# A gated hybrid layer on one core: memory tokens as the first stage, x normalized before its only split, cross heads ahead of causal heads

## The chip, the core and the metric

The kernel runs on one of the eight cores of a Trainium2 chip. TensorE (PE in the profile, its weight loads PEld) multiplies; VectorE (DVE), ScalarE (ACT) and GpSimd (POOL) do the rest; SyncE (SP) issues nearly all the DMAs. Each engine takes its own instructions in the order in which the program emits them and waits on semaphores for the others. The metric is the device time of one execution in microseconds (us), and less is better.

## The reference

One decoder layer with three parallel branches, for 256 tokens `x` and 256 memory tokens `mem`, 1024 channels each, all float32:

```python
h = rms_norm(x, norm_g)
(qa, ka, va, ga, ub, vb, gb, qc, gc, ma, mb, mc) = split_cols(h @ w_in, IN_SPLITS)
out_a = moba_attention(rope(qa), rope(ka), va) * silu(ga)            # 6 causal heads x 128
out_b = ub * (tril(w_spatial) @ layer_norm(vb) + b_spatial) * silu(gb)   # 6 groups, chunks of 128 tokens
mem_n = rms_norm(mem, mem_norm_g)
mk, mv = split(mem_n @ w_mem_kv)
out_c = softmax(qc @ mk.T * scale) @ mv * silu(gc)                   # 4 cross heads x 128
y = (sigmoid(ma) * (out_a @ w_branch_a) + sigmoid(mb) * (out_b @ w_branch_b)
     + sigmoid(mc) * (out_c @ w_branch_c))
return rms_norm(x + y @ w_out, final_norm_g)
```

With 256 tokens and blocks of 256 the block-sparse attention is one causal block for each head.

## The kernel before, in words

**Arithmetic.** Nearly every product is made of three matmuls on numbers of reduced width (`mm3`, L343): an operand is split into a high part, rounded on ScalarE, and a low part, the rest, on VectorE, and high x high, high x low and low x high are summed in PSUM.

**Chunks.** All weights pass through TensorE as 106 chunks of 128x1024, two of which make a piece of 1 MB that is one load (L168 to L176). `plan` (L46) gives the order of the first 82. A *token* chunk (vvb, mv, sig; `mm_tok`) holds two k-slices of 512 columns and takes 12 matmuls; four of them make one group of 512 output columns with tokens on the partitions. A *feature* chunk (q, k, qc, gc, ub, ga, gb, mk; `mm_fea`, matmuls on L435) holds all eight k-slices of 128 columns and takes 16 matmuls; its result has features on the partitions. vvb is the causal heads' v beside the gMLP's v, sig the merge gates. Then come 16 chunks of branch projections (`mm_br`) and 8 of the output projection (`mm_out`).

**Loop.** The loop at L983 runs over the chunks. In turn `c` it first emits side work (`U.slot(c, False)`), then the split of chunk `c + 3` (`split`: high part L184, low part L188), maybe a load on SP, then the matmuls of chunk `c`, and then side work for TensorE (`U.slot(c, True)`). Raw pieces have three buffers, split chunks four.

**Planner.** `Units` (L68) holds the side work as units with an engine, a supposed duration, what they come after, and a due turn. It keeps a supposed clock for each engine. A unit is emitted when it seems ready and its engine is not too far ahead of TensorE, or at the latest in its due turn. It sets only the order of emission; what really holds an engine is the semaphores.

**First stage.** L224 to L228 load `xw`: for each of eight k-slices, 256 columns of transposed x and 512 of weights (ten DMAs, `st` tiles). L229 to L237 then load pieces 2 and 3 and x by rows (`load_x`). The lines 307 to 319 multiply x by its gain without its norm, split that as `hh`, `hl`, and split the weights; the first four chunks, vvb 0, run on these (L375). The rows' norm comes from the squares of x (`xsq0`, `xsq1`, L268), square root, reciprocal, two diagonals that two matmuls with a matrix of ones spread over the partitions (`rms_all`, L288), and a copy to SBUF. For vvb it is applied when the sums leave PSUM (`evict_v`). For all later chunks GpSimd multiplies transposed x by it (`nm0` to `nm7`, L516), and each k-slice is split a second time with the gain (`nxh`, `nxl`).

**Memory tokens.** They are loaded after x's norm is known (`load_mem`), split with their gain in units `mxh`, `mxl`, and used by mk and mv as chunks 46 to 53; their norm is applied to mk by a multiplication (`mkf`) and to mv when it leaves PSUM.

**Heads.** Each head is a chain of units: scores on TensorE, maximum on VectorE, exponent on ScalarE, normalization, a turn of the weights (by VectorE's 32x32 transposes for causal heads 2 and 3 and cross heads 0 to 2, L571, on TensorE for the others), split, product with v, copy. `back` lets a head start only when the third head before it is normalized. Six causal heads come first, then four cross heads.

Of the kernel before, what the change touches and what calls it, by code (L numbers as in the profile page):

```python
# [45 lines left out]
def plan():  # L46


    p = [("vvb", g) for g in range(3)]
    for r in range(3):  # L50
        p += [(n, h) for h in (2 * r, 2 * r + 1) for n in ("q", "k")]
        p += ([("sig", 0)], [("gc", h) for h in range(HC)], [("ga", h) for h in range(4)])[r]
        p += [("ub", 2 * r + i) for i in range(2)]
    p += [(n, h) for n in ("qc", "mk") for h in range(HC)]
    p += [("mv", 0), ("sig", 1)]
    p += [("ga", h) for h in range(4, HA)]
    p += [("gb", g) for g in range(GB)]
# [70 lines left out]
def tile_hybrid_layer(ctx: ExitStack, tc: tile.TileContext, xw, memT, mem, x, fin_g, ln_g, w, w_sp, b_sp, rope, out):  # L128
# [108 lines left out]
    load_x()  # L237

# [27 lines left out]
    def row_squares(src, acc, junk):  # L266

        nc.scalar.activation(junk, src, AF.Square, accum_out=acc)  # L268
# [38 lines left out]
    for k in range(KD):  # L307
        c, a, g = k // 2, (k % 2) * 512, gain[:, k:k + 1]
        if k in (0, 2):

            nc.vector.tensor_scalar(hh[:, k, :], x_k(k), g, None, op0=OP.mult)
        elif k < 4:
            gain_hi(x_k(k), g, hh[:, k, :])
        for o, e in (((0, 256), (256, 512)) if k == 0 else ((0, 512),)):
            nc.scalar.activation(hi[c][:, a + o:a + e], st_k(k, S + o, S + e), AF.Copy)  # L315
# [44 lines left out]
    def mm_tok(c):  # L360
        _, name, o, k0 = chunks[c]
        sh, sl = {"mv": ("mh", "ml"), "sig": ("nh", "nl")}.get(name, (None, None))
        sh, sl = (V[sh], V[sl]) if sh else (hh, hl)
# [18 lines left out]
        if k0 + 2 == KD and name == "vvb":  # L382
            U.add(f"vvb.{o}", ACT, 1.6, lambda: evict_v(o), after=[f"vvb.{o - 512}" if o else "xrow", f"c{c}"],
                  first=True)
# [12 lines left out]
        elif k0 + 2 == KD:  # L397
            slot_tile("mvl", [128, 2, CW], "mr0", F32R)
            for t in range(2):
                p, f = acc[name, o][t], rstm[:, t:t + 1]  # L400
                h, l = V["cx"][:, 2, 2 * t:2 * t + 2, :].rearrange("p a b -> p (a b)"), V["mvl"][:, t, :]
                nc.scalar.activation(h, p, AF.Copy, scale=f)
                U.run(ACT, 0.62, U.end[f"c{c}"])
                later(f"mvl{t}", DVE, 0.7, scaled_lo, l, p, f, h, due=c + 2)
            U.end[f"{name}.{o}"] = U.end[f"c{c}"]

    def evict_v(o):
# [708 lines left out]
```

## Time and profile before

| | |
|---|---|
| time, two runs | 325.04 and 324.62 us, median 324.83 us |
| span of the profiled execution, first to last instruction | 323.3 us |
| the profiled execution's own time | not given apart from its span; the runs' median stands 1.5 us above the span |
| busy: TensorE, weight loads | 315.8 us (98%), 268.9 us (83%) |
| busy: VectorE, ScalarE, GpSimd | 246.6 us (76%), 202.5 us (63%), 40.1 us (12%) |
| moved by DMA | 64.92 MB, mean 201 GB/s, 400 to 430 GB/s from 8 to 26 us |
| mean granted TensorE clock | 0.998 |

The profile is of one execution. A row of a listing in order of time gives start, duration, engine, line, operation, the tile written and the tiles read, shapes, count, and in brackets how long the engine stood idle before it and what ended that. A row of waits gives waiter and releaser, then total, times and longest in us. A row of windows gives the stretch, then busy time of TensorE, weight loads, VectorE, ScalarE and GpSimd with instruction counts, the granted clock, the DMA's busy share and its GB/s.

### The profile page before, as it was taken

Reading aid. Unit: us, or ns where it says so; the run is one execution under the profiler, and the core shown is the slowest. Engines: PE = TensorE matmul, PEld = TensorE weight load, DVE = VectorE, ACT = ScalarE, POOL = GpSimd, SP = SyncE. Lnnn points to the kernel's source line nnn. Section 1 sums busy time; section 2 is a strip of 40 time slices with the busy share of each in tenths; the row PEclk is TensorE's granted clock in tenths of the full one; section 3 lists DMA queues with packets and bytes.
Section 4 is the critical chain, followed back from the end, with each engine's and each line's share of the span. In section 5 each row is a group of like instructions: output and inputs, shape, how many; then the busy total and the mean of one; then the engine's idle time right before and its main releaser. Section 6 shows DMA issues by size and latency. Waiting matters only on the chain.

```text
span 323.3 us, 4570 instructions
## 1 busy us (share of the span) xinstructions
PE 315.8 (98%) x1644; PEld 268.9 (83%) x1644; DVE 246.6 (76%) x419; ACT 202.5 (63%) x346; POOL 40.1 (12%) x42
## 2 busy tenths in 40 slices
PE   8999999999999999999999999999999999999992
PEld 3788888888888888898888888888888888888982
DVE  3969956985876999898979639989857659769452
ACT  4879887556865555557677698576746633434433
POOL 1007420000000000030200009200124000000022
PEclk9999999999999999999999999999999999999999
DMA  7999796555327565554544533864640667463003
GB/s 246 419 426 398 258 363 220 216 194 216 136 78 302 172 180 208 164 192 138 185 151 176 195 130 131 312 233 170 208 182 19 244 231 289 150 241 130 0 2 130
DMA packets 13846, 64.92 MB, mean 201 GB/s; under 512 B 1792, under 2 KB 2944, under 8 KB 8576
## 3 DMA queue, kind: packets, MB, share of 16 engines
q1 hardware_dynamic: 13536, 64.31, 55.1%
q10 hardware_dynamic: 288, 0.33, 0.3%
q8 instruction: 13, 0.21, 0.2%
q14 instruction: 9, 0.07, 0.1%
HBM read 62.79 MB, written 1.05 MB: 197 GB/s over the span
## 4 chain that ended last, share of the span: by engine, by line
PE 96%; DMA 2%; ACT 1%; SPq 0%; ACTq 0%; issue 0%; DVE 0%
PE acc L435 36%; PE acc L344 13%; PE acc L345 13%; PE acc L346 13%; PE aux L344 5%; PE aux L345 5%; PE aux L346 5%; PE acc L375 3%; DMA st<-in_xw_dram 2%; PE aux L579 1%; PE aux L814 1%; PE aux L626 0%; PE aux L674 0%; SPq L218 0%; ACT hi L315 0%; PE aux L288 0%
## 5 line engine op out<-in xcount | busy, mean ns | idle before, releaser
L188 DVE TENSOR_TENSOR lo<-raw,hi 128x1024 fp32r<-128x1024 f32 x102 | 130.2, 1280 | 43.0 <-ACT hi L184 42.0
L184 ACT ACTIVATE hi<-raw 128x1024 fp32r<-128x1024 f32 x102 | 107.6, 1056 | 44.3 <-PE acc L346 29.6
L435 PE MATMUL acc<-n,hi 128*128 128x512 f32 x304 | 78.5, 394 | 0.0
L435 PEld LDWEIGHTS acc<-n,hi 128*128 128x128 f32 x304 | 54.8, 189 | 9.5
L435 PEld LDWEIGHTS acc<-n,lo 128*128 128x128 f32 x304 | 41.5, 190 | 3.0
L435 PE MATMUL acc<-n,lo 128*128 128x256 f32 x304 | 42.4, 282 | 0.0
L344 PE MATMUL acc<-hi,n 128*128 128x512 f32 x80 | 31.5, 394 | 0.0
L345 PE MATMUL acc<-lo,n 128*128 128x512 f32 x80 | 31.2, 390 | 0.0
L346 PE MATMUL acc<-hi,n 128*128 128x512 f32 x80 | 31.2, 389 | 0.0
L571 DVE STREAM_TRANSPOSE mid<-p 32x128 f32<-32x128 f32 (+1 forms) x80 | 23.1, 289 | 1.6 <-ACT p L609 0.5
L741 POOL TENSOR_TENSOR vb<-vb,lng 128x768 f32<-128x768 f32 x2 | 4.6, 2276 | 108.4 <-DMA raw<-in_w_dram 94.7
L346 PEld LDWEIGHTS acc<-hi,n 128*128 128x128 f32 x80 | 15.0, 188 | 3.2
L345 PEld LDWEIGHTS acc<-lo,n 128*128 128x128 f32 x80 | 15.0, 188 | 2.9
L344 PEld LDWEIGHTS acc<-hi,n 128*128 128x128 f32 x80 | 15.0, 188 | 2.9
L958 POOL TENSOR_TENSOR xk<-xk,fing 128x512 f32<-128x512 f32 (+1 forms) x4 | 4.0, 1013 | 68.0 <-ACT jk L954 68.0
L516 POOL TENSOR_TENSOR st<-st,bc 128x256 f32<-128x256 f32 x8 | 9.1, 1170 | 24.4 <-ACT bc L293 24.4
L439 ACT ACTIVATE qk<-acc 128x256 f32<-128x256 f32 x12 | 4.6, 380 | 10.7 <-PE acc L435 10.6
L439 ACT ACTIVATE jt<-acc 128x256 f32<-128x256 f32 x14 | 5.3, 377 | 9.0 <-PE acc L435 8.9
L825 POOL TENSOR_TENSOR qk<-qk,ga 128x512 f32<-128x512 f32 x3 | 5.8, 1966 | 33.8 <-ACT ga L801 33.8
L375 PE MATMUL acc<-hi,h 128*128 128x512 f32 (+1 forms) x34 | 8.9, 386 | 0.9 <-ACT hi L315 0.9
L344 PE MATMUL acc<-hi,a 128*128 128x512 f32 x24 | 9.4, 393 | 0.0
L346 PE MATMUL acc<-hi,a 128*128 128x512 f32 x24 | 9.3, 389 | 0.0
(233 smaller groups left out, 601.2 us busy)
## 6 DMA issues: line engine op xcount, KB each, us to landing
raw<-in_w_dram SPq DMA_DIRECT2D x39, 1024.0 KB, 4.9
raw<-in_w_dram SPq DMA_DIRECT2D x24, 512.0 KB, 4.6
st<-in_xw_dram SPq DMA_DIRECT2D x6, 384.0 KB, 7.2
xk<-in_x_dram SPq DMA_DIRECT2D x2, 1024.0 KB, 9.1
mt<-in_memT_dram SPq DMA_DIRECT2D x2, 512.0 KB, 7.8
mm<-in_mem_dram SPq DMA_DIRECT2D x2, 512.0 KB, 9.8
out_dram<-xk SPq DMA_DIRECT2D x4, 256.0 KB, 2.7
fing<-in_fin_g_dram SPq DMA_DIRECT2D x1, 512.0 KB, 6.9
```

The source lines that it names most:

```text
L184: nc.scalar.activation(hi[c][:, a:b], raw[c // 2][:, o + a:o + b], AF.Copy)
L188: nc.vector.tensor_tensor(lo[c][:, a:b], raw[c // 2][:, o + a:o + b], hi[c][:, a:b].bitcast(F32), OP.subtract)
L344: nc.tensor.matmul(p, s_hi, m_hi, start=first, stop=False)
L345: nc.tensor.matmul(p, s_hi, m_lo, start=False, stop=False)
L346: nc.tensor.matmul(p, s_lo, m_hi, start=False, stop=last)
L375: nc.tensor.matmul(acc[name, o][t][:, a:b], src[:, k, tsl(t)], wt[c][:, i * 512 + a:i * 512 + b], start=k + n == 0, stop=k == KD - 1 and n ...
L435: nc.tensor.matmul(o, wt, m, start=i == 0, stop=i == len(passes) - 1)
L439: nc.scalar.activation(dst, pa, AF.Copy)
L516: U.add(f"nm{k}", POOL, 1.05, lambda k=k: nc.gpsimd.tensor_tensor(x_k(k), x_k(k), bc["x"], OP.mult), after=["xrms"], due=7)
L571: nc.vector.transpose(dst(slice(32 * b, 32 * b + 32), slice(32 * a, 32 * a + 32)), src(slice(32 * a, 32 * a + 32), slice(32 * b, 32 * b + ...
L741: nc.gpsimd.tensor_tensor(V["vb"][:, t, :], V["vb"][:, t, :], V["lng"], OP.mult)
L825: nc.gpsimd.tensor_tensor(src, src, g, OP.mult)
```

## The change

1. **Order of chunks.** mv and mk, the memory tokens' values and keys, are chunks 0 to 7; then vvb, then qc, then the causal heads' q and k with sig 0, gc, sig 1 and ub between them, ga, gb and the rest of sig.
2. **First stage.** The first eight k-slices bring transposed mem in place of transposed x (`mw` for `xw`). The first four chunks are mv 0; their sums wait in PSUM until mem's row norm is known (`evict_mv`).
3. **Loads.** On SP, behind the k-slices, come x by rows, pieces 2 and 3, transposed x in two halves, piece 4, and mem by rows. Before, it was pieces 2 and 3, x by rows, piece 4, and mem only later.
4. **x is split once.** The squares of x are due in turn 1. Transposed x is multiplied by gain and norm: for k-slices 0 to 3 in one VectorE operation that reads the norm from PSUM, for 4 to 7 by the gain on ScalarE and by the norm on GpSimd. Then two k-slices at a time are split (`nx0` to `nx3`, due in turns 6 to 9). vvb now reads this split, and its sums leave PSUM without a factor, in the turn in which they end.
5. **Memory's splits** as units of their own (`mxh`, `mxl`) are gone.
6. **Heads.** The four cross heads stand ahead of the six causal heads in the planner's list and in `back`.

```diff
 def plan():
-    p = [("vvb", g) for g in range(3)]
+    p = [("mv", 0)] + [("mk", h) for h in range(HC)] + [("vvb", g) for g in range(3)]
+    p += [("qc", h) for h in range(HC)]
     for r in range(3):
         p += [(n, h) for h in (2 * r, 2 * r + 1) for n in ("q", "k")]
-        p += ([("sig", 0)], [("gc", h) for h in range(HC)], [("ga", h) for h in range(4)])[r]
+        p += ([("sig", 0)], [("gc", h) for h in range(HC)], [("sig", 1)])[r]
         p += [("ub", 2 * r + i) for i in range(2)]
-    p += [(n, h) for n in ("qc", "mk") for h in range(HC)]
-    p += [("mv", 0), ("sig", 1)]
-    p += [("ga", h) for h in range(4, HA)]
+    p += [("ga", h) for h in range(HA)]
...
+    load_x()
     raw_alloc(2)
     load_part(2, 0, CH)
     load_part(2, CH, PIECE)
     load(3)
-    load_x()
+    slot_tile("xt", [128, KD, S], "mr")
+    for i in range(2):
+        nc.sync.dma_start(V["xt"][:, 4 * i:4 * i + 4, :], xT[:, 4 * i:4 * i + 4, :])
+    load(4)
+    for t, g in enumerate(("och", "ocl")):
+        slot_tile(f"mm{t}", [128, D], g)
+        nc.sync.dma_start(V[f"mm{t}"], mem[:, t, :])
...
-            acc[name, o] = [bank(), bank()] if o == 1024 else [acc_bank(), acc_bank()]
+            acc[name, o] = [bank(), bank()] if (name, o) == ("vvb", 0) else [acc_bank(), acc_bank()]
...
-            U.add(f"vvb.{o}", ACT, 1.6, lambda: evict_v(o), after=[f"vvb.{o - 512}" if o else "xrow", f"c{c}"],
-                  first=True)
+            evict_v(c, o)
...
+            U.add("mve", ACT, 1.25, evict_mv, after=["mrow", f"c{c}"], first=True)
...
-    U.end["load_x"] = 18.5
+    U.end["load_x"], U.end["load_xt"], U.end["load_mem"] = 12.8, 20.5, 26.0
     for t in range(2):
-        U.add(f"xsq{t}", ACT, 1.25, ..., after=["load_x"], due=5)
-    U.chain("xrow", *rms_rows(ssx, rstd, rts[:, 0:2]), after=["xsq0", "xsq1"], due=5)
-    U.chain("xrms", *rms_all("x", rstd), after=["xrow"], due=[5, 6, 7])
+        U.add(f"xsq{t}", ACT, 1.25, lambda t=t: row_squares(V["xk"][:, t, :], ssx[:, t:t + 1]),
+              after=["load_x"], due=1)
+    U.chain("xrow", *rms_rows(ssx, rstd, rts[:, 0:2]), after=["xsq0", "xsq1"], due=2)
+    U.chain("xrms", *rms_all("x", rstd), after=["xrow"], due=[2, 4, 5])
+    def norm_k(k):
+        z = V["xt"][:, k, :]
+        nc.vector.scalar_tensor_tensor(z, z, gains[:, k:k + 1], bc["px"][:, 0:S], op0=OP.mult, op1=OP.mult)
...
+        if k < 4:
+            U.add(f"nm{k}", DVE, 0.42, lambda k=k: norm_k(k), after=["xrms.1", "load_xt"], due=5)
+        else:
+            U.add(f"ng{k}", ACT, 0.42, lambda k=k: norm_gain(k), after=["load_xt"], due=5)
+            U.add(f"nm{k}", POOL, 1.2, lambda k=k: nc.gpsimd.tensor_tensor(
+                V["xt"][:, k, :], V["xt"][:, k, :], bc["x"], OP.mult), after=["xrms", f"ng{k}"], due=6)
+    for i in range(KD // 2):
+        U.chain(f"nx{i}", (ACT, 0.62, lambda i=i: norm_hi(i)), (DVE, 0.7, lambda i=i: norm_lo(i)),
+                after=[f"nm{2 * i}", f"nm{2 * i + 1}"], due=6 + i)
...
-        return [] if n < 0 else [f"a{stage}{n}" if n < HA else f"c{stage}{n - HA}"]
+        return [] if n < 0 else [f"c{stage}{n}" if n < HC else f"a{stage}{n - HC}"]
...
-            U.end[f"s{s}"] = U.run(DVE, 1.23, U.run(ACT, 1.05, max(U.end.get(f"c{s - SPL}", 0), 9.0 + 1.45 * s)))
-        if s % 2 == 1 and 3 < s // 2 + 2 < n_pieces:
+            came = {2: 15.0, 3: 18.0, 4: 24.0, 5: 28.5}.get(s // 2, 0.0)
+            U.end[f"s{s}"] = U.run(DVE, 1.23, U.run(ACT, 1.05, max(U.end.get(f"c{s - SPL}", 0), came)))
+        if s % 2 == 1 and 4 < s // 2 + 2 < n_pieces:
```

`U.end["load_x"]` and `came` are the planner's supposed landings in us, which only order the emission.

More of the change, by code (lines that the diff above doesn't have):

```diff
@@ L127, in tile_hybrid_layer @@
 @with_exitstack
[L128 removed]
+def tile_hybrid_layer(ctx: ExitStack, tc: tile.TileContext, mw, xT, mem, x, fin_g, ln_g, w, w_sp, b_sp, rope, out):
     nc = tc.nc
@@ L397, in mm_tok, with cross_tile, evict_mv, evict_v @@
         elif k0 + 2 == KD:
[L398 to L407, printed above, removed]
+            U.add("mve", ACT, 1.25, evict_mv, after=["mrow", f"c{c}"], first=True)
+    def cross_tile():
+        if "cx" not in V:
+            slot_tile("cx", [128, 3, HC, S], "p2", F32R)
+    def evict_mv():
+        cross_tile()
+        slot_tile("mvl", [128, 2, CW], "ga", F32R)
+        for t in range(2):
+            p, f = acc["mv", 0][t], rstm[:, t:t + 1]
+            h, l = V["cx"][:, 2, 2 * t:2 * t + 2, :].rearrange("p a b -> p (a b)"), V["mvl"][:, t, :]
+            nc.scalar.activation(h, p, AF.Copy, scale=f)
+            later(f"mvl{t}", DVE, 0.7, scaled_lo, l, p, f, h, due=now[0] + 2)
+    def evict_v(c, o):
         if o == 0:
@@ L412, in evict_v @@
         for t in range(2):
-            p, f = acc["vvb", o][t], rstd[:, t:t + 1]
+            p = acc["vvb", o][t]
             n = max(0, min(512, AW - o))
@@ L514, in tile_hybrid_layer @@
-    U.chain("xrms", *rms_all("x", rstd), after=["xrow"], due=[5, 6, 7])
-    for k in range(KD):
-        U.add(f"nm{k}", POOL, 1.05, lambda k=k: nc.gpsimd.tensor_tensor(x_k(k), x_k(k), bc["x"], OP.mult),
-              after=["xrms"], due=7)
-    for k in range(KD):
-        U.add(f"nxh{k}", ACT, 0.42, lambda k=k: gain_hi(x_k(k), gain[:, k:k + 1], V["nh"][:, k, :]),
-              after=[f"nm{k}", "nxa"], due=8 + k // 2)
-        U.add(f"nxl{k}", DVE, 0.5, lambda k=k: gain_lo(x_k(k), gain[:, k:k + 1], V["nh"][:, k, :], V["nl"][:, k, :]),
-              after=[f"nxh{k}"], due=8 + k // 2)
@@ L523, in tile_hybrid_layer @@
-    U.add("consts", POOL, 1.3, setup_consts, after=[f"nm{KD - 1}"], wait=4.0)
-    def load_mem():
-        for i in range(2):
-            slot_tile(f"mt{i}", [128, KD // 2, S], f"mr{i}")
-            nc.sync.dma_start(V[f"mt{i}"], memT[:, 4 * i:4 * i + 4, :])
-        for t, g in enumerate(("och", "ocl")):
-            slot_tile(f"mm{t}", [128, D], g)
-            nc.sync.dma_start(V[f"mm{t}"], mem[:, t, :])
-    def mem_alloc():
-        pair("m", "x2", KD)
-    def mem_k(k):
-        return V[f"mt{k // 4}"][:, k % 4, :]
@@ L546, in load_fin @@
+    U.add("gmlp", POOL, 1.6, setup_gmlp, after=["vvb.0"], wait=8.0)
     def load_fin():
@@ L845, in tile_hybrid_layer @@
     sig2 = chunks.index(("tok", "sig", 1024, 6))
-    U.add("oaTa", None, 0, lambda: pair("a", "x2", HA), after=["mv.0"])
+    U.add("oaTa", None, 0, lambda: pair("a", "x2", HA), after=["c7"])
     for i in range(3):
```

162 lines of the change are left out of this document (79 added, 83 removed).

## The prediction

> **What bounds the kernel now.** I read the page first (busy shares, slices, chain), then the waits of TensorE, then the first 45 us in order of time, engine by engine, and last the tail in short windows.
>
> ```profile
> PE 315.8 (98%) x1644; PEld 268.9 (83%) x1644; DVE 246.6 (76%) x419; ACT 202.5 (63%) x346; POOL 40.1 (12%) x42
> PE 96%; DMA 2%; ACT 1%; SPq 0%; ACTq 0%; issue 0%; DVE 0%
> ```
>
> ```profile
> PE acc L375 <- ACT hi L315: 0.9, 1, 0.9
> PE aux L250 <- PEq L1105: 0.8, 1, 0.8
> ```
>
> TensorE (PE) is busy 315.8 of 323.3 us, and the chain that ends last runs through it for 96%. Its waits are two, 1.7 us in all, both in the first 9 us. From 8.35 us on it is never seen waiting:
>
> ```profile
> 8.35 8.48 PE acc L375 x36
> ...
> 38.84 11.15 PE acc L435 x64
> ...
> 317.59 0.25 ACT jk L954
> ```
>
> So the kernel is a string of matmuls from 8.35 to about 317.5 us, with a head of 8 us and a tail of 6 us. What can come off is at most the idle 323.3 - 315.8 = 7.5 us, all in head and tail; what can be added is any place where something now reaches TensorE late. So I count the matmuls first, and then look for late operands.
>
> **The matmuls.** The plan has the same 82 chunks in another order: 12 of vvb, 4 of mv, 24 of sig and 42 of 128 columns. The first four keep the short form (50 matmuls, L375), now on memory tokens. Ten heads keep their products, their turns (three cross heads and two causal heads on VectorE) and their order of passes; each of the two row norms keeps its two broadcast matmuls (L288). Sum: 1644 before and 1644 after, 0.0 us. The head reads the same layout (a k-slice of the 256 tokens beside 512 weight columns) through the same ten DMAs, so 0.85 to 8.35 us stays. The tail after the last matmul isn't edited.
>
> **The queue of loads is where the change reaches the path.** SP issues the two halves of piece 2 (L170) from 5.29 us, piece 3, and then x. In the new order x stands ahead of piece 2, and after piece 3 come xT, piece 4 and mem. These rows of ScalarE (ACT) and SP give the landings:
>
> ```profile
> 8.62 0.33 SPq L235 DMA_DIRECT2D xk<-in_x_dram  x1
> ```
>
> ```profile
> 13.05 0.50 ACT L300 ACTIVATE h<-st,st 128x256 fp32r<-128x256 f32 x1
> 13.87 1.06 ACT L184 ACTIVATE hi<-raw 128x1024 fp32r<-128x1024 f32 x1 [0.33 <-DMA raw<-in_w_dram]
> 15.12 1.06 ACT L184 ACTIVATE hi<-raw 128x1024 fp32r<-128x1024 f32 x1 [0.19 <-DMA raw<-in_w_dram]
> 17.61 2.01 ACT L184 ACTIVATE hi<-raw 128x1024 fp32r<-128x1024 f32 x2 [1.43 <-DMA raw<-in_w_dram]
> 20.01 1.06 ACT L268 ACTIVATE jx<-xk 128x1024 f32<-128x1024 f32 x1 [0.39 <-DMA xk<-in_x_dram]
> 22.02 0.18 ACT L268 ACTIVATION_READ_ACCUMULATOR jx<-xk 128x1 f32 x1
> 22.29 0.30 ACT L273 ACTIVATE rts<-ssx,eps 128x2 f32<-128x2 f32 x1
> 22.57 1.06 ACT L184 ACTIVATE hi<-raw 128x1024 fp32r<-128x1024 f32 x1
> ```
>
> Each of these waits ended with a landing: half of piece 2 at 13.9, all of it at 15.1, piece 3 at 17.6, x at 20.0. That is 1.05 MB every 2.5 us, the rate that the DMA holds throughout:
>
> ```profile
> 12.00:14.00 2.00, 2.00 (x11) 1.65 (x10) 2.00 (x5) 1.67 (x5) 0.00 (x0) 1.00 1.05 432
> ...
> 18.00:20.00 2.00, 2.00 (x10) 1.66 (x9) 1.30 (x2) 1.62 (x2) 0.00 (x0) 1.00 1.02 430
> ```
>
> (430 GB/s in the last column.) Each megabyte takes its predecessor's place: x at 15.1, half of piece 2 at 16.4, all of it at 17.6, piece 3 at 20.0, then by 2.5 us each xT 22.5, piece 4 25.0, mem 27.5, piece 5 30.0.
>
> **Chunk 4, the one stall that I put on the path.** Today its first matmul runs without a gap at 16.67, its weights' high part (hi, L184) having been ready since 14.93:
>
> ```profile
> 16.67 0.39 PE L344 MATMUL acc<-hi,h 128*128 128x512 f32 x1
> ```
>
> In the new order the squares of x (`xsq0`, `xsq1`) are due at slot 1, and slot 1 is emitted before the split of chunk 4. ScalarE takes its queue in order, so behind the end of the prelude (13.55) stand: squares, waiting for x until 15.1; then 2.19 us for the two (20.01 to 22.20 above), to 17.3; then the split of chunk 4, 1.06, to 18.35. Chunk 4 is now mk 0, which needs that high part with its first matmul. What waits behind the squares on ScalarE is thus just the split that TensorE wants next. Stall: 18.35 - 16.67 = 1.7 us. Without the squares the weights alone, half of piece 2 at 16.4, would give 16.4 + 1.06 = 17.5, a stall of 0.8. Bounds: 0.0 if x lands by 13.4 (squares to 15.6, split to 16.67, if its half piece is there), and 2.6 if x lands 0.9 later, sharing the engines with the half piece behind it. I take 1.7, as the row at 15.12 is a landing of the same byte count from the same place in the queue.
>
> VectorE (DVE) follows: low part of chunk 4, reciprocal, diagonals, low part of chunk 5. The low part of chunk 4 is wanted after seven long passes: 16 matmuls of a 128-column chunk take 11.15 / 4 = 2.79, the long ones 0.23, so 1.6 after 18.35, at 19.95; it is there at 18.35 + 1.2 = 19.6. Nothing is added.
>
> **Chunk 8, the normalized x.** The vvb chunks used to read unnormalized x with the norm in the eviction; now they need x normalized and split, which puts a new chain ahead of TensorE. These rows price it (the last four fields of the third are shapes and counts):
>
> ```profile
> 22.62 0.17 DVE L274 RECIPROCAL rstd<-rts 128x2 f32<-128x2 f32 x1 [1.56 <-ACT rts L273]
> 24.07 1.22 DVE L188 TENSOR_TENSOR lo<-raw,hi 128x1024 fp32r<-128x1024 f32 x1
> 28.59 0.74 DVE L349 SCALAR_TENSOR_TENSOR v<-acc,rstd,v 128x512 fp32r<-128x512 f32 x1
> 31.06 1.76 DVE L188 TENSOR_TENSOR lo<-raw,hi 128x1024 fp32r<-128x1024 f32 x1
> 36.57 0.86 DVE L303 SCALAR_TENSOR_TENSOR n<-st,st,n 128x256 fp32r<-128x256 f32 x2
> ```
>
> ```profile
> 26.09 9.09 POOL L516 TENSOR_TENSOR st<-st,bc 128x256 f32<-128x256 f32 x8 [24.45 <-ACT bc L293]
> ```
>
> ```profile
> L349 DVE SCALAR_TENSOR_TENSOR mvl<-acc,rstm,cx x2: 744/748/752, 163.8 to 164.5; 128x512 fp32r<-128x512 f32 x2
> L303 DVE SCALAR_TENSOR_TENSOR n<-st,n x4: 936/955/965, 29.3 to 33.6; 128x256 fp32r<-128x256 f32 x4
> ```
>
> ```profile
> L352 DVE TENSOR_TENSOR mkl<-jt,cx x2: 684/684/685, 154.5 to 155.1; 128x512 fp32r<-128x512 f32 x2
> ```
>
> ```profile
> L441 DVE TENSOR_TENSOR qk<-qk,acc x12: 411/414/422, 42.7 to 111.7; 128x256 f32<-128x256 f32 x12
> ```
>
> While GpSimd multiplied (26.1 to 35.2) an operation on two SBUF tensors took 1.76 instead of 1.22; one that reads PSUM took 0.74, as it does alone (0.748). The four products on VectorE (`norm_k`) read the broadcast from PSUM, so I price them at 0.45 (two of this shape in 0.86), not at the 0.955 of the slowed row. GpSimd's four take 9.09 / 8 = 1.14 each, about 23.3 to 28.0. VectorE from 18.35 on: low parts of 4, 5, 6 at 1.2, of 7 and 8 at 1.76 beside GpSimd, reciprocal and diagonals 24.07 - 22.62 = 1.45, joins of mk 0 and 1 at 0.41, four products 1.8, first low pair of x 0.68: 3.6 + 3.5 + 1.45 + 0.8 + 1.8 + 0.7 = 11.9, to 30.2. Chunk 8 begins at 18.35 + 4 x 2.79 + 0.24 (broadcast) = 29.75 and wants the low pair two matmuls later, 30.2. Covered to the tenth: 0.0, with bounds of 1.1 to spare (low parts not slowed) and 2.0 late (products slowed to 0.955). After that each chunk of 2.73 brings VectorE 1.2 + 0.4 + 0.7 = 2.3, so it doesn't fall further back. The squares of mem (2.19 on ScalarE, due from 27.5) stand between splits made three chunks ahead; 0.0.
>
> **What goes.** The second and third split of a 256-row (8 and 8 ScalarE instructions of 0.5, 16 of VectorE at 0.47 to 0.955) shrink to four of each at 512 columns and four products; GpSimd's eight products become four. That takes some 3 to 5 us from ScalarE, VectorE and GpSimd each, none of which ended a wait of TensorE after 9 us: 0.0.
>
> **Cross heads first.** The same steps at another time. The tightest step seen before a product is here:
>
> ```profile
> L352 DVE TENSOR_TENSOR ptl<-aux,pth x2: 416/416/417, 165.1 to 165.5; 128x256 fp32r<-128x256 f32 x2
> ```
>
> ```profile
> L345 PE MATMUL aux<-ptl,v x2: 279/280/281, 166.4 to 167.7; 128*128 128x256 f32 x2
> ```
>
> 0.5 us of slack from 165.9 to 166.4. The planner's clock had TensorE at chunk 4 at 4.5 + 4 x 2.73 = 15.4 and the chip was there at 16.67, 1.25 later; now it plans 15.4 + 1.05 + 1.23 = 17.7 against my 18.35, 0.65 later. Steps lose 0.6 of slack at most, and each stall gives it back, so all of them together cost 0 to 0.6; I take 0.
>
> **Sum.** 0.0 + 1.7 + 0.0 + 0.0 + 0.0: span 323.3 + 1.7 = 325.0. The two runs' median 324.83 stands 1.5 above the profiled span, so the time is 326.5.
>
> **Rivals.**
> - *No stall* (0.12): x and piece 2 land 1.7 us earlier than the slots that I gave them, the squares are hidden. Against: the DMA already moves 430 GB/s. Time 324.8.
> - *A second stall at chunks 8 to 11* (0.18): VectorE has no spare time there; products at 0.955 add 2.0, and an xT that lands later than 25.6 adds its lateness. 327.5 to 330, by the middle 328.5.
> - *Slower by over 2%* (0.06): x lands no sooner than today. The squares block ScalarE until 22.2, the split ends at 23.3, and TensorE idles 6.6 us. Then its clock goes too. After the last matmul, at 317.55, these windows (the clock is third from the end) hold it full for some 4.3 us and then halve it, and half speed is the 0.43 us per matmul of the warm-up against 0.23:
>
> ```profile
> 317.00:318.00 1.00, 0.55 (x5) 0.35 (x3) 0.60 (x2) 0.54 (x4) 1.00 (x2) 1.00 0.00 0
> ...
> 321.00:322.00 1.00, 0.00 (x0) 0.00 (x0) 0.00 (x0) 0.00 (x0) 0.00 (x0) 0.92 0.49 152
> 322.00:323.00 1.00, 0.00 (x0) 0.00 (x0) 0.00 (x0) 0.00 (x0) 0.00 (x0) 0.50 0.00 0
> ```
>
> ```profile
> 0.84 3.57 PE L250 MATMUL aux<-const-bfloat16-1.0 128*128 128x512 bf16 x8 [0.84 <-PEq L1105]
> ```
>
> Eight at that rate lose 1.6, so 324.8 + 6.6 + 1.6 = 333.0. It decides from an x later than 18.3 on. Against: SP issues x before piece 2, and the queue has kept its order so far. The Trainium skill ("TensorE: Matmul & The Clock Gate", the section on HAM oscillation) puts the idle time that costs the clock at about 3.4 us. By it an x from 16.8 on would cost the 1.6 as well; the tail here shows 4.3. My stall of 1.7 keeps the clock by either.
> - *Faster by over 2%* (0.02): 6.5 us would have to come from 7.5 of idle head and tail, neither edited.
>
> **How the numbers follow.** The forecast, one stall of 0.8 to 2.6 with its own range 325.5 to 327.5, has 0.62. Range 324.8 to 329.2: it leaves out half of the first rival, the top of the second, and the last two, about 2 in 10. Within 2% (318.3 to 331.3, about what a measurement of this kernel can tell from no change) lie forecast, no stall and second stall: 0.62 + 0.12 + 0.18 = 0.92; slower 0.06, faster 0.02.
>
> **What would show it.** In the changed kernel's profile: 1644 matmuls; one new wait of TensorE on ScalarE's hi at about 16.7 us, some 1.7 long; the squares of x on ScalarE between the prelude and the first L184, begun near 15.1 after a wait for x; no wait at chunk 8 near 29.8, with VectorE solid from 18 to 30; no wait later over 0.6 in sum. Wrong it would be with a chunk 4 that starts at 16.7 or after 19.3, a second wait on VectorE or GpSimd at chunks 8 to 11, waits at the heads' products, or a matmul count that differs.

## The result, and the profile after

| | before | after |
|---|---|---|
| time, two runs, median | 324.83 us | 328.63 us (328.49 and 328.78) |
| ratio after / before | | 1.0116, 95% interval 1.0087 to 1.0146 |
| span of the profiled execution | 323.3 us | 326.9 us |
| first matmul of chunk 4 | 16.67 us | 18.13 us |
| start of the last matmul | 317.27 us | 320.49 us |

The change made the kernel 3.8 us slower. The forecast was 1.7 us slower, and 328.63 lies inside its range (324.8 to 329.2), though above the 325.5 to 327.5 that it gave to its own mechanism. In a later set of runs the same kernel took 327.97 us, ratio 1.0100 [1.0085, 1.0115].

The page of the changed kernel has these lines in answer to those of before (engines with their share of the span, and the chain of work that ended last):

```profile
span 326.9 us, 4543 instructions
...
PE 317.5 (97%) x1644; PEld 269.7 (83%) x1644; DVE 240.4 (74%) x411; ACT 201.2 (62%) x340; POOL 34.6 (11%) x38
...
PE 89%; DMA 7%; ACT 1%; DVE 1%; ACTq 0%; issue 0%
```

The matmuls are 1644 as before. VectorE lost 6.2 us of work, ScalarE 1.3, GpSimd 5.5, and none of it shortened the span. What changed is the chain: before it was TensorE from 8.35 us on; now it runs through DMA until 25 us. TensorE's waits say where (total, times, longest):

```profile
PE acc L446 <- ACT hi L183: 1.3, 1, 1.3
PE acc L446 <- DVE jt L452: 1.0, 2, 0.7
PE aux L256 <- PEq L1110: 0.8, 1, 0.8
```

The third was there before. The first was forecast. The second, two waits of a feature chunk's matmuls (L446) on VectorE's join of an mk (L452), was not. TensorE in order of time, the first passes and the last matmul of chunks 4 to 7 (start, duration, and the idle time before in brackets):

```profile
18.13 1.89 PE L446 MATMUL acc<-m,hi 128*128 128x512 f32 x7 [1.30 <-ACT hi L183]
...
23.83 0.39 PE L446 MATMUL acc<-m,hi 128*128 128x512 f32 x1
24.57 1.90 PE L446 MATMUL acc<-m,hi 128*128 128x512 f32 x7 [0.35 <-DVE jt L452]
...
27.27 0.40 PE L446 MATMUL acc<-m,hi 128*128 128x512 f32 x1
28.33 1.88 PE L446 MATMUL acc<-m,hi 128*128 128x512 f32 x7 [0.67 <-DVE jt L452]
...
31.23 0.40 PE L350 MATMUL aux<-hi,n 128*128 128x512 f32 x1
```

A long pass is followed by the next matmul 0.23 us after it started. The brackets count idle time only after the modelled end of the matmul before, so I go by starts:

- Chunk 4: 18.13 - 16.67 = 1.46 us late.
- Chunk 6: 24.57 instead of 23.83 + 0.23 = 24.06, 0.51 lost.
- Chunk 7: 28.33 instead of 27.27 + 0.23 = 27.50, 0.83 lost.
- After each of the three waits the first seven passes take 1.9 where chunk 5, which follows without one, took 1.78: about 0.1 each time, 0.35 in all over the three chunks.
- No wait after chunk 7.

Together 1.46 + 0.51 + 0.83 + 0.35 = 3.15 us, of the 3.22 by which the last matmul starts later. The rest of the span's 3.6 us lies behind that matmul. From the start of the last matmul to GpSimd's last semaphore clear it is 5.7 us in both (317.27 to 323.0, 320.49 to 326.2); from the clear to the end of the span it is 0.3 before and 0.7 after.

**Chunk 4** went as forecast. ScalarE in the changed kernel:

```profile
14.94 1.06 ACT L274 ACTIVATE xk<-xk 128x1024 f32<-128x1024 f32 x1 [1.46 <-DMA xk<-in_x_dram]
...
17.04 1.04 ACT L183 ACTIVATE hi<-raw 128x1024 fp32r<-128x1024 f32 x1
...
25.09 1.06 ACT L183 ACTIVATE hi<-raw 128x1024 fp32r<-128x1024 f32 x1 [0.77 <-DMA raw<-in_w_dram]
...
42.83 1.26 ACT L414 ACTIVATE cx<-acc,rstm 128x512 fp32r<-128x512 f32 x2
```

ScalarE stood still for x until 14.94, squared it, and only at 17.04 began the split that TensorE needed; it ended at 18.08.

**Chunks 6 and 7.** The last of those rows is `evict_mv`, which empties the sums of mv 0 at 42.8 us, when memory's norm is known. PSUM is handed out in two sets of four banks: `acc_bank` for running sums and `bank` (tiles `aux`) for everything else. mv 0 is two accumulators of `acc_bank`, full at 16.8 and held until 42.8. That leaves two banks for mk 0 to 3: mk 0 and mk 1 take them, and mk 2 (chunk 6) can begin only when the bank of mk 0 has been read by ScalarE's copy and VectorE's join, mk 3 when that of mk 1 has. The joins stand in VectorE's queue:

```profile
20.69 3.49 DVE L187 TENSOR_TENSOR lo<-raw,hi 128x1024 fp32r<-128x1024 f32 x3
24.10 0.42 DVE L452 TENSOR_TENSOR jt<-jt,acc 128x256 f32<-128x256 f32 x1
24.43 1.65 DVE L529 SCALAR_TENSOR_TENSOR xt<-xt,gains,aux 128x256 f32<-128x256 f32 x4
26.18 1.77 DVE L187 TENSOR_TENSOR lo<-raw,hi 128x1024 fp32r<-128x1024 f32 x1
27.87 0.41 DVE L452 TENSOR_TENSOR jt<-jt,acc 128x256 f32<-128x256 f32 x1
28.20 0.68 DVE L358 TENSOR_TENSOR n<-xt,n 128x512 fp32r<-128x512 f32 x1
```

The join of mk 0, whose last matmul began at 20.79, runs at 24.10 behind the low parts of chunks 5, 6 and 7, and chunk 6 starts as it ends. The join of mk 1 runs at 27.87 behind the low part of chunk 8, and that waited for a landing, as the chain shows:

```profile
11.48 13.52 DMA raw<-in_w_dram
...
25.09 1.07 ACT hi L183
...
26.18 1.77 DVE lo L187
27.95 0.34 DVE jt L452
...
28.33 3.07 PE acc L446 x16
```

So chunk 7 waited for the landing of a weight piece (piece 4, chunks 8 and 9) that it doesn't read, because a bank that it needs was to be emptied by an instruction behind the split of that piece. In this execution the landing and VectorE's own work tie: the four products (L529) ended at 26.08, and the low part behind them could start at 26.18. VectorE (third pair of numbers) was busy for 10.61 of the 11 us from 18 to 29:

```profile
18.00:29.00 11.00, 9.86 (x53) 8.15 (x54) 10.61 (x18) 9.38 (x18) 4.82 (x7) 1.00 1.02 416
```

This is the theory after the result: the banks make TensorE wait for the joins, and the joins come late by what stands ahead of them in VectorE's queue. The rival: TensorE waits at chunks 6 and 7 since VectorE is overloaded by the products of x (L529), and would wait there with any banks.

### The profile page after: what moved, and what is told of

It is laid out like the page before. It is cut to its first block, busy times and chain, and to the rows that moved or that the text cites. A ratio compares the mean times of both kernels' runs of the same rounds, so it can differ in the third digit from the quotient of the medians.

```text
span 326.9 us, 4543 instructions
## 1 busy us (share of the span) xinstructions
PE 317.5 (97%) x1644; PEld 269.7 (83%) x1644; DVE 240.4 (74%) x411; ACT 201.2 (62%) x340; POOL 34.6 (11%) x38
## 4 chain that ended last, share of the span: by engine, by line
PE 89%; DMA 7%; ACT 1%; DVE 1%; ACTq 0%; issue 0%
PE acc L446 33%; PE acc L350 14%; PE acc L351 14%; PE acc L352 14%; DMA raw<-in_w_dram 4%; PE aux L352 4%; PE aux L351 4%; PE aux L350 4%; DMA st<-in_mw_dram 3%; PE aux L597 1%; PE aux L818 1%; DVE lo L187 1%; PE aux L644 0%; PE aux L692 0%; ACT hi L183 0%; ACT xk L979 0%
## 5 line engine op out<-in xcount | busy, mean ns | idle before, releaser
L187 DVE TENSOR_TENSOR lo<-raw,hi 128x1024 fp32r<-128x1024 f32 x102 | 128.1, 1258 | 53.4 <-ACT hi L183 52.0
L446 PE MATMUL acc<-n,hi 128*128 128x512 f32 x304 | 78.5, 393 | 0.0
L446 PEld LDWEIGHTS acc<-n,hi 128*128 128x128 f32 x304 | 54.8, 189 | 9.4
L350 PE MATMUL acc<-hi,n 128*128 128x512 f32 x128 | 50.2, 392 | 0.0
L352 PE MATMUL acc<-hi,n 128*128 128x512 f32 x128 | 49.9, 390 | 0.0
L351 PE MATMUL acc<-lo,n 128*128 128x512 f32 x128 | 49.8, 389 | 0.0
L446 PEld LDWEIGHTS acc<-n,lo 128*128 128x128 f32 x304 | 41.4, 190 | 3.0
L446 PE MATMUL acc<-n,lo 128*128 128x256 f32 x304 | 42.3, 282 | 0.0
L352 PEld LDWEIGHTS acc<-hi,n 128*128 128x128 f32 x128 | 24.0, 188 | 5.1
L351 PEld LDWEIGHTS acc<-lo,n 128*128 128x128 f32 x128 | 24.0, 188 | 4.8
L350 PEld LDWEIGHTS acc<-hi,n 128*128 128x128 f32 x128 | 24.0, 188 | 4.7
L446 PE MATMUL acc<-m,hi 128*128 128x512 f32 x32 | 9.0, 404 | 2.3 <-ACT hi L183 1.3
L380 PE MATMUL acc<-hi,m 128*128 128x512 f32 (+1 forms) x34 | 9.7, 415 | 0.1
L351 PE MATMUL acc<-lo,a 128*128 128x512 f32 x24 | 9.3, 389 | 0.0
## 6 DMA issues: line engine op xcount, KB each, us to landing
xt<-in_xT_dram SPq DMA_DIRECT2D x2, 512.0 KB, 11.9
```

Of the source, the lines that this page charges most:

```text
L187: nc.vector.tensor_tensor(lo[c][:, a:b], raw[c // 2][:, o + a:o + b], hi[c][:, a:b].bitcast(F32), OP.subtract)
L350: nc.tensor.matmul(p, s_hi, m_hi, start=first, stop=False)
L351: nc.tensor.matmul(p, s_hi, m_lo, start=False, stop=False)
L352: nc.tensor.matmul(p, s_lo, m_hi, start=False, stop=last)
L380: nc.tensor.matmul(acc[name, o][t][:, a:b], src[:, k, tsl(t)], wt[c][:, i * 512 + a:i * 512 + b], start=k + n == 0, stop=k == KD - 1 and n ...
L446: nc.tensor.matmul(o, wt, m, start=i == 0, stop=i == len(passes) - 1)
```

## The experiments

**mv 0's sums in the other set of banks.** One line; vvb 0 then takes main banks.

```diff
-            acc[name, o] = [bank(), bank()] if (name, o) == ("vvb", 0) else [acc_bank(), acc_bank()]
+            acc[name, o] = [bank(), bank()] if (name, o) == ("mv", 0) else [acc_bank(), acc_bank()]
```

> The sums of mv 0 go to two banks of the pool for side work, those of vvb 0 to the main pool; nothing else. Theory (mv holds two of the four main banks, so that chunks 6 and 7 wait until VectorE has joined mk 0 and mk 1): the two waits on the join, 1.0 us on TensorE and some 0.4 us of refill behind them, go, chunk 4 stays at 18.1, the time falls from 328.6 by 1.4 to 1.7, to about 327.0. Rival (VectorE is simply behind from 18 to 30 us): the wait comes back at chunk 8, on a low part, and the time stays at 328.3 to 328.8.

Measured: 326.47 us, ratio 1.0060 [1.0037, 1.0082]. TensorE's waits, beside the one from before the first matmul:

```profile
PE acc L446 <- ACT hi L183: 1.0, 1, 1.0
```

Chunks 6 and 7 run on without a gap (each row of eight is the last matmul of one chunk and the first seven of the next):

```profile
22.94 2.00 PE L446 MATMUL acc<-m,hi 128*128 128x512 f32 x8
...
25.73 2.00 PE L446 MATMUL acc<-m,hi 128*128 128x512 f32 x8
```

Both waits on the join are gone with VectorE's work unchanged (10.70 us busy from 18 to 29); the theory holds and the rival falls. Chunk 4, which this line doesn't touch, began at 17.23 here and at 18.13 in the first profile; in the repeat of the changed kernel (below) it began at 17.36, with the landings as early as here. So part of the difference in time is that of the loads: the banks are worth 328.63 - 326.47 = 2.2 us by the two medians, and 1.5 us against the repeat's 327.97; by the ratios, since the sets ran on different chips, 1.8 and 1.3. The traces say 1.6: from the start of chunk 4 to the start of the last matmul it is 302.4 us in both profiles of the changed kernel (18.13 to 320.49, 17.36 to 319.76) and 300.8 here (17.23 to 318.04).

**Squares of x two turns later.** They then stand behind the splits of chunks 4 and 5.

```diff
-              after=["load_x"], due=1)
+              after=["load_x"], due=3)
-    U.chain("xrow", *rms_rows(ssx, rstd, rts[:, 0:2]), after=["xsq0", "xsq1"], due=2)
-    U.chain("xrms", *rms_all("x", rstd), after=["xrow"], due=[2, 4, 5])
+    U.chain("xrow", *rms_rows(ssx, rstd, rts[:, 0:2]), after=["xsq0", "xsq1"], due=3)
+    U.chain("xrms", *rms_all("x", rstd), after=["xrow"], due=[3, 5, 6])
```

> The squares of x, the square root and the diagonals are due in turn 3 instead of 1 and 2, behind the splits of chunks 4 and 5, the broadcast one turn later; loads and banks as in the changed kernel. Theory: chunk 4 waits only for its half of piece 2, which stands behind x: split 16.3 to 17.4, wait 0.7 instead of 1.5. But the reciprocal and the diagonals then stand on VectorE behind the squares (done at about 20.7) and ahead of the low parts of chunks 6 and 7 and of the join of mk 0, which ends near 25.2, while chunk 6 could start at 22.9: its wait grows from 0.5 to about 2.2. Time 328.3 to 329.0, no gain. Rival (the waits are independent, the one at chunk 4 is the squares' alone): 327.8.

Measured: 329.19 us, 1.0127 [1.0103, 1.0152]; the profiled execution took 327.92, the other three 329.12 to 329.32, so the median, 0.2 over what was expected, is 1.3 us above what these rows show. The mean granted clock was 0.999 in the profiled execution and 0.992 in the other three, lower than in any other run here but the next experiment's; no trace shows where they lost it. TensorE and VectorE:

```profile
16.96 1.89 PE L446 MATMUL acc<-m,hi 128*128 128x512 f32 x7 [0.58 <-ACT hi L183]
...
24.87 1.88 PE L446 MATMUL acc<-m,hi 128*128 128x512 f32 x7 [1.80 <-DVE jt L452]
```

```profile
22.13 2.35 DVE L187 TENSOR_TENSOR lo<-raw,hi 128x1024 fp32r<-128x1024 f32 x2
24.40 0.41 DVE L452 TENSOR_TENSOR jt<-jt,acc 128x256 f32<-128x256 f32 x1
```

Chunk 4 began 1.17 us earlier than in the first profile (18.13 to 16.96), but 0.45 of that is the loads, which SP issued earlier here (piece 4 at 11.03, there at 11.48). Its wait, counted from where TensorE would have gone on (0.46 us after the start of the last pair of matmuls before it), was 0.73 us (16.23 to 16.96) instead of 1.46. Either way the squares are some 0.7 us of the wait, as theory had it; what is left is the load order. But nothing came off the time. The join of mk 0 runs at 24.40, behind the diagonals of x's norm and the low parts of chunks 6 and 7, and all of these stand behind the squares, which ScalarE ended at 20.25; so chunk 6 began at 24.87, hardly later than in the changed kernel (24.57), having waited 1.8 instead of 0.35. A wait is moved, not removed: while the banks are held, TensorE's place at chunk 6 is set by what stands ahead of the join, not by the start of chunk 4.

**x loaded behind piece 3.** This makes the rival of a much later x true.

```diff
-    load_x()
     raw_alloc(2)
     load_part(2, 0, CH)
     load_part(2, CH, PIECE)
     load(3)
+    load_x()
```

> x by rows is loaded behind piece 3, as before the change; the squares stay due in turn 1. The forecast's rival of more than 2%: x lands at 20.0, the squares hold ScalarE until 22.2, the split of chunk 4 ends at 23.3, TensorE stands idle for 6.6 us, and its granted clock halves after some 4 us of that and costs 1.6 more; with the waits at chunks 6 and 7 as they are the time is 324.8 + 6.6 + 1.6 + 1.6 = 334.6. If ScalarE's order didn't hold the split back, the time would be 327 and chunk 4 would start at 16.7. If idle time of this length did not cost the clock, 333.0.

Measured: 333.40 us, 1.0266 [1.0239, 1.0293]. ScalarE and TensorE:

```profile
19.58 1.06 ACT L274 ACTIVATE xk<-xk 128x1024 f32<-128x1024 f32 x1 [6.48 <-DMA xk<-in_x_dram]
```

```profile
22.77 3.35 PE L446 MATMUL acc<-m,hi 128*128 128x512 f32 x7 [6.27 <-ACT hi L183]
```

TensorE idled for 6.3 us and lost its clock (columns: the stretch; busy time and instructions of TensorE, weight loads, VectorE, ScalarE, GpSimd; granted clock; share and GB/s of the DMA):

```profile
18.00:20.00 2.00, 0.00 (x0) 0.00 (x0) 0.00 (x0) 0.42 (x1) 0.00 (x0) 1.00 0.99 406
20.00:22.00 2.00, 0.00 (x0) 0.00 (x0) 0.00 (x0) 2.00 (x5) 0.00 (x0) 0.52 1.05 430
...
24.00:26.00 2.00, 2.00 (x6) 1.52 (x6) 1.82 (x6) 1.74 (x2) 0.00 (x0) 0.50 0.97 389
26.00:28.00 2.00, 2.00 (x13) 1.93 (x12) 2.00 (x3) 0.26 (x1) 0.00 (x0) 0.77 0.31 53
```

The seven long passes took 3.35 instead of 1.89, the chunk 4.77 instead of 2.90. So the dearest rival was sound in mechanism and size (333.0 in the prediction, 333.4 here); only its condition was not met, since the queue brought x at 14.9. What this run's own expectation added, 1.6 us of waits at chunks 6 and 7, did not come: the pieces had landed meanwhile, and the join of mk 0 ran at 28.74, before TensorE came for the bank at 30.56.

**Three edits together**: mv 0 in the other banks, x between piece 2 and piece 3, squares two turns and the broadcast one turn later. The first and third as above, and

```diff
-    load_x()
     raw_alloc(2)
     load_part(2, 0, CH)
     load_part(2, CH, PIECE)
+    load_x()
     load(3)
```

> Three edits together: mv 0 in the side pool's banks, x loaded between pieces 2 and 3, its squares due in turn 3 and the broadcast one turn later. Theory: chunk 4 starts at 16.7 without a wait (its split at 13.9), chunks 6 and 7 find free banks; left is 0 to 1.0 at chunk 8, whose normalized x is ready at about 28.5 against a start at 28.1. Time 324.8 to 326.0. If memory tokens ahead, the heads' order or the single split cost something of their own later on, the time stays above 326.5.

Measured: 326.74 us, 1.0062 [1.0043, 1.0081]. No wait at chunks 4, 6 or 7, but a new one at chunk 8, the first to read x:

```profile
28.69 0.50 PE L350 MATMUL acc<-hi,n 128*128 128x512 f32 x1 [0.63 <-ACT n L538]
```

```profile
25.64 1.23 DVE L187 TENSOR_TENSOR lo<-raw,hi 128x1024 fp32r<-128x1024 f32 x1 [1.94 <-ACT hi L183]
27.11 1.65 DVE L529 SCALAR_TENSOR_TENSOR xt<-xt,gains,aux 128x256 f32<-128x256 f32 x4
```

With the broadcast a turn later the products of x are emitted after the low part of chunk 8, and VectorE, which takes its queue in order, idled 1.9 us for that chunk's weights before it reached them. The expectation of 324.8 to 326.0 missed this by 0.7. It is the rival of chunk 8 in the prediction, made true by an edit, and by the order of the queue, not by the amount of work.

**The changed kernel again**, beside the runs that follow, as their yardstick.

> The changed kernel itself once more, beside the next three on the same chip: ratio 1.010 to 1.013 to the kernel before, with waits at chunks 4 (1.3 to 1.5), 6 (0.5) and 7 (0.8).

Measured: 327.97 us, 1.0100 [1.0085, 1.0115]. Waits at the same three places, by the starts 1.04, 0.51 and 0.86 us long; the one at chunk 4 is under the 1.3 to 1.5 that was expected, since x came 0.77 earlier and TensorE was free only 0.35 earlier (16.32 instead of 16.67). Chunk 4 came at 17.36, chunk 6 at 23.80 and chunk 7 at 27.57, each 0.77 earlier than in the first profile, the last matmul 0.73 earlier, at 319.76. The loads were earlier too. The issue of piece 4 on SP, in the first profile and in this one:

```profile
11.48 0.33 SPq L169 DMA_DIRECT2D raw<-in_w_dram  x1
```

```profile
10.71 0.33 SPq L169 DMA_DIRECT2D raw<-in_w_dram  x1
```

In the first profile SP was 0.77 later with the same issues, x landed at 14.94 against 14.17 and piece 4 at 25.09 against 24.38, and the whole kernel followed. This is the chain's DMA share seen from another side: up to chunk 7 the changed kernel goes by its loads.

**All products of x on GpSimd**, so that VectorE is relieved of 1.65 us and the rival of the overloaded VectorE gets its test from the other side, with the banks unchanged.

```diff
     for k in range(KD):
-        if k < 4:
+        if k < 0:
```

> All eight products of x with its norm on GpSimd, with the gain on ScalarE; VectorE is rid of its four (1.65 us at 24.4). Theory: the join of mk 1 stands on VectorE behind the low part of chunk 8, which can't start before piece 4 has landed (25.1) and been rounded (26.15); so the join still ends near 28.3, chunk 7 still waits 0.7 to 1.0, chunk 6 0.5, and the time is that of the changed kernel within 0.4, or up to 0.6 more as VectorE's low parts are slowed for longer. Rival (the four products are what makes VectorE late): chunk 7's wait goes and the time falls by 0.8 to 0.9.

Measured: 329.00 us, 1.0128 [1.0113, 1.0143]: slower, with less on VectorE. TensorE at chunk 7, and VectorE before it:

```profile
28.75 1.88 PE L446 MATMUL acc<-m,hi 128*128 128x512 f32 x7 [1.42 <-DVE jt L452]
```

```profile
26.51 1.85 DVE L187 TENSOR_TENSOR lo<-raw,hi 128x1024 fp32r<-128x1024 f32 x1 [2.29 <-ACT hi L183]
```

VectorE stood idle for 2.29 us and the wait at chunk 7 still grew. The eight gains on ScalarE (22.2 to 25.5) put the high part of chunk 8 off to 25.4, and the join behind the low part of chunk 8 went with it. With 1.65 us of work less, the join came no sooner, since its place in the queue is behind a split that waits. The edit is not a clean test of VectorE's load, as it moves the wait to ScalarE; that test is the run with the other banks. The run is 1.0 slower than its yardstick, more than the 0.6 that was allowed.

**One of the two squares on VectorE** (with mv 0 in the other banks), to shorten what stands ahead of chunk 4's split.

```diff
+    def squares_dve(z, acc):
+        nc.vector.tensor_tensor_reduce(z, z, z, 1.0, 0.0, OP.mult, OP.add, acc)
+
+    U.add("xsq0", ACT, 1.25, lambda: row_squares(V["xk"][:, 0, :], ssx[:, 0:1]), after=["load_x"], due=1)
+    U.add("xsq1", DVE, 1.25, lambda: squares_dve(V["xk"][:, 1, :], ssx[:, 1:2]), after=["load_x"], due=1)
```

> mv 0 in the side pool's banks, and the squares of the second 128 rows of x on VectorE, which is idle from 14.8 to 18.1; loads and turns as in the changed kernel. Theory: chunk 4's wait has two parts, the second square (1.06 with its read) and then the half piece that x was put ahead of. ScalarE gets to the split at about 16.1, the half piece is there at 15.9 to 16.2, the split ends near 17.2: wait 0.4 to 0.7 instead of 1.5, time 0.8 to 1.0 under the run with only the banks exchanged, 325.4 to 325.8. Rival (the wait at chunk 4 is the load order's alone): no change from 326.5.

Measured: 326.06 us, 1.0035 [1.0021, 1.0048], 0.4 below the run that moved mv 0 alone (0.8 by the ratios, since the two ran on different chips) and 0.3 over the top of what was expected. ScalarE and TensorE:

```profile
16.10 1.06 ACT L183 ACTIVATE hi<-raw 128x1024 fp32r<-128x1024 f32 x1 [0.20 <-DMA raw<-in_w_dram]
```

```profile
17.21 1.89 PE L446 MATMUL acc<-m,hi 128*128 128x512 f32 x7 [0.61 <-ACT hi L183]
```

The split of chunk 4 now ends its wait with the landing of its weights: the part that is left is the load order. Chunk 4 started where it did in the run that moved mv 0 alone (17.23), with x landing 0.70 later here (14.74 against 14.04); by its own wait it is 0.76 us here (16.45 to 17.21) and 1.20 there. The intervals of the two times overlap, so that it is the traces that show the gain. The prediction had 17.5 for that case, 0.8 late.

**And x between the halves of piece 2**, so that chunk 4's own weights come first; squares due one turn later. Beside the two edits above:

```diff
-    load_x()
     raw_alloc(2)
     load_part(2, 0, CH)
+    load_x()
     load_part(2, CH, PIECE)
```

> As the run with a square on VectorE, and besides x is loaded between the two halves of piece 2, and its squares are due in turn 2, behind the split of chunk 4. Theory: chunk 4 finds its weights at 14.9 and doesn't wait; the diagonals end at about 19.3, the broadcast after chunk 4 waits 0.0 to 0.2; chunk 8's x is ready at about 28.9 against a start at 28.1 and a need at 28.5, a wait of 0 to 0.5. Time 324.9 to 325.6: the changed order costs nothing of its own once its waits are gone, and gains nothing either, as the count of matmuls is the same. If it fell under 324.0 the matmuls would not be the bound.

Measured, in ten runs: 325.48 us, 1.0024 [1.0013, 1.0034]. TensorE no longer waits at chunks 4 to 8; the largest gap left, about 0.2 us, is the second of these rows (the matmul ahead of it began at 33.34 and 0.23 is a step):

```profile
16.18 1.75 PE L446 MATMUL acc<-m,hi 128*128 128x512 f32 x7
...
33.76 0.50 PE L352 MATMUL acc<-hi,n 128*128 128x512 f32 x1
```

From the start of chunk 4 to the start of the last matmul it is 301.1 us (16.18 to 317.29) against 300.6 in the kernel before (16.67 to 317.27). In the two runs that give mv 0 the other banks and leave the loads alone the same stretch took 300.8. So once the banks and ScalarE's queue are put right, memory first, one split of x and cross heads first, with the edits that put them right, cost 0.2 to 0.5 us between them behind the start of chunk 4, and earn nothing: the interval of the times lies wholly above the kernel before, by 0.4 to 1.1 us.

The tail of this profile shows how soon the clock can fall. TensorE's last matmul ended at 317.57, and by this window (clock third from the end) the clock was full until 319.52, 1.95 us later:

```profile
319.00:320.00 1.00, 0.00 (x0) 0.00 (x0) 0.48 (x2) 0.56 (x2) 0.00 (x0) 0.76 0.00 0
```

**The same with mv 0 back in the main banks.** If the three waits were separate, this would be about 327.1; if chunks 6 and 7 follow the landings whenever chunk 4 starts, 327.9 to 328.4.

```diff
-            acc[name, o] = [bank(), bank()] if (name, o) == ("mv", 0) else [acc_bank(), acc_bank()]
+            acc[name, o] = [bank(), bank()] if (name, o) == ("vvb", 0) else [acc_bank(), acc_bank()]
```

> As the run with x between the halves of piece 2 and a square on VectorE, but mv 0 again in two of the four main banks and vvb 0 in the side pool, as in the changed kernel. Theory: chunk 4 still starts without a wait, but chunk 6 then comes for its bank at 21.8, and the join of mk 0 stands on VectorE behind the low parts of chunks 6 and 7, which follow the landing of piece 3, and ends at 23.4 whatever TensorE does: wait 1.5. Chunk 7 comes at 26.2, the join of mk 1 ends at 27.2: wait 1.0. Time 2.4 to 2.9 above the run without held banks, 327.9 to 328.4, no better than the changed kernel. Rival (the waits at chunks 4, 6 and 7 are separate prices): 1.6 above it, 327.1.

Measured: 328.03 us, 1.0093 [1.0076, 1.0110]. TensorE, and VectorE's joins:

```profile
24.20 1.89 PE L446 MATMUL acc<-m,hi 128*128 128x512 f32 x7 [1.21 <-DVE jt L452]
...
28.05 1.88 PE L446 MATMUL acc<-m,hi 128*128 128x512 f32 x7 [0.78 <-DVE jt L452]
```

```profile
23.74 0.41 DVE L452 TENSOR_TENSOR jt<-jt,acc 128x256 f32<-128x256 f32 x1
...
27.59 0.41 DVE L452 TENSOR_TENSOR jt<-jt,acc 128x256 f32<-128x256 f32 x1
```

Chunk 4 began at 16.49 without a wait, and the time is that of the changed kernel (327.97). All that was won there was lost again at chunks 6 and 7. Between this kernel and that of the run above it lies one line, worth 328.03 - 325.48 = 2.55 us by the medians and 0.0069 x 324.8 = 2.2 by the ratios, as they ran on two chips; from the start of chunk 4 to the start of the last matmul it is 303.7 us (16.49 to 320.21) against 301.1.

**The kernel before again**, for one profile of it from a later chip, on account of the close of the span.

> The kernel before once more, for its profile's two ends: 324.3 to 325.3. If the changed kernels' longer close (6.1 us from the end of the last matmul, against 5.8 in the one profile of before) belongs to the kernels, it is 5.8 here too; if it varies by execution, anything from 5.7 to 6.2.

Measured: 325.18 us, span 323.3, and 5.8 us from the end of the last matmul to the end of the span, as in the first profile. In the ten profiles of a kernel with the new order it is 6.1 to 6.2.

What was not tried: the order of the heads by itself. Heads of both kinds have to be done before the branch projections, and cross heads first presupposes mk, mv and qc at the front. That it costs nothing rests on the changed kernel's trace alone, where TensorE waits nowhere after chunk 7.

## Why the prediction was right or wrong

- **Direction and range right, under half the size.** +1.7 us was forecast, +3.8 measured (+3.2 in the repeat, by its ratio). A time within 2% had 0.92 and came. That the range held is in part luck: it was stretched over half of the rival of a second stall, whose mechanism did not come, and the forecast's own range for one stall, 325.5 to 327.5, was missed by 0.5 (repeat) to 1.1 us.
- **Matmul count, head, savings, heads first: 0.0 each.** As forecast. 1644 matmuls; less work on three engines without a microsecond gained; no wait late in the kernel. What all of it may cost together is the 0.2 to 0.5 us above, which no run parts.
- **Chunk 4, 1.7 us: right.** 1.46 measured, with x at 14.94 (forecast 15.1) and the split at 17.04 to 18.08 (forecast 17.3 to 18.35). In the repeat chunk 4 started 0.7 after the 16.67 of before, having waited 1.04; both lie within the bounds of 0 to 2.6. The forecast's parting into squares and load order (1.7 with, 0.8 without the squares) is borne out by the waits: 0.73 with the later squares, 0.76 with the shared squares, against 1.04 to 1.53 in the four profiles where both squares stand ahead and x comes before piece 2. What it lacked is 0.1 for TensorE's restart.
- **Chunk 8, 0.0: right.** Its first matmul came at 31.23, 1.5 later than forecast, but the first low pair of x was there at 28.88, early enough for the forecast's start at 29.75 too. VectorE was as solid with work as the balance had it (10.61 of 11 us). The work was a little less than its 11.9 us: the four products took 1.65, priced at 1.8, and GpSimd slowed only one low part (1.77). What the balance didn't ask is which instruction of that solid queue TensorE needs first: not the pair of x, but a join.
- **The step that failed** is the sum's list of terms at chunks 5 to 7: "VectorE (DVE) follows ... Nothing is added." It asked of each chunk whether its operands were ready, and never whether its result had a place to go. The line that says so was in the diff that the prediction had before it: mv 0 gets main banks and keeps them until memory's norm. With four banks, two held and one for each mk, the third mk must wait for the first's join, and that join's place is given by VectorE's queue: 20.69 + 3.49 for the first; for the second the landing of piece 4 at 25.09 plus split, low part and join, with the products ahead of that low part ending only 0.1 us sooner. 0.51 + 0.83, with 0.25 of restarts some 1.6 us, was the missing term in the first profile. The one-line experiments put it at 1.3 to 2.2 as the change stands (1.6 by the traces), and at 2.2 to 2.6 where chunk 4 is on time, since TensorE then arrives sooner at joins that don't.
- **Rivals.** The time of the *second stall* (327.5 to 330, mid 328.5) is what came, but not by its mechanism nor its place: it was to come at chunks 8 to 11 from VectorE's products. Relieving VectorE of the products made the kernel slower; giving mv 0 other banks, with the products kept, took the stall away. *No stall* is refuted, *faster* too. *Slower by over 2%* has been made true by loading x later: 333.4 against 333.0.
- **The clock.** In that run TensorE's last matmul ended at 16.5 and the windows hold the clock full to 20.0 and at 0.52 from 20.0 to 22.0, so it fell at about 20.1, after 3.6 us of idle time; in the tail of before it held 4.3. The prediction took 4.3 for a limit, and it is one sample. In the tail of the run with x between the halves of piece 2 it held 1.95, in that of the run with the squares two turns later 5.2 (0.66 in the window from 325 to 326, the last matmul having ended at 320.10). The Trainium skill ("TensorE: Matmul & The Clock Gate", "What's actually happening") gives about 3.4 us for the window and calls it free-running, so that one program may find it at different phases. A spread from 1.95 to 5.2 us, about one such window wide, agrees with that; but 3.4 us of idle time is no safe limit here, as 1.95 after the last matmul was enough once. A wait of 1.8 us in mid kernel kept the clock in the one profile that has it.
- **The close of the span**, 0.3, was no term of the sum ("the tail isn't edited"). In the first profiles it lies behind GpSimd's last clear, but with all products on GpSimd only 0.4 lies behind it and the rest ahead, and no run shows the cause.

## What to carry to other kernels

Before an order of work is changed, count for each stage where its sums will lie and until when, as well as when its operands come: a sum that waits for a late scale is a bank taken out of the ring, and the next stages then wait for the instruction that empties theirs, wherever that stands in its engine's queue. Ask of each instruction on an in-order queue what it may wait for, and what stands behind it: here a split that waited for a DMA held up a join of 0.4 us, and so a chunk that needed nothing of that DMA. Such waits don't add up: with the wait at chunk 4 taken away alone, the next ones grew by as much, while freeing the banks alone was worth 1.6 us. So look first for the wait that the others run into.

## What the runs showed that was not expected

- SP's issue of the same loads comes up to 0.9 us later in one execution than in another (piece 4 issued at 10.57 to 11.48 in the six profiles with the changed kernel's loads). The changed kernel's time follows it nearly one for one (0.77 at chunk 7, 0.73 at the last matmul, for 0.77 of SP). Both profiles of the kernel before have it at the same place (9.58 and 9.54), so they don't show what it does there.
- A restart of TensorE after a wait costs by itself: the seven long passes after each of the three waits took 1.88 to 1.90 us, against 1.75 to 1.78 where there was none. The clock was full in both cases.
- An operation that reads PSUM beside one operand in SBUF was not seen slowed by GpSimd: a join took 0.42 while GpSimd multiplied and 0.41 after it, and four products 1.65 beside it, while a low part, with two operands in SBUF, went from 1.23 to 1.77.
- After the 6.3 us of idle time the clock was at 0.50 until 26 and at 0.77 in the mean of 26 to 28. Half speed until t and full speed after it give 0.77 for t = 26.9: 4.1 us after the matmuls resumed, which cost 1.9 us in chunk 4.
- The first matmuls of the prelude took longer in some executions (six in 2.05 us at 4.24 in the changed kernel and at 4.39 in the repeat of the kernel before) than in others (1.25 in the first profile of before), as at half speed: the traces' record of the clock starts, at full, at 4.41 us in that profile and at 6.34 and 6.63 in these two (windows ahead of it read 1.00 for lack of a record). The time didn't change: the matmuls of the next k-slices to land began at 8.34, 8.30 and 8.35 all the same.
